# A decoder block on one core: down-projection terms at other places of the slot order, and four of eight weight sums of a unit made by accumulating DMAs

## The chip, the core and the metric

The kernel runs on one core of a Trainium2 chip. The metric is the device time of one execution in microseconds, as the median over runs of the same program. A profile of one further execution gives the time of every instruction on the five engines: PE (TensorE, matrix products, with PEld for its weight loads), ACT (ScalarE), DVE (VectorE), POOL (GpSimd) and SP (SyncE, which here issues the loads).

## The reference

One decoder layer over 256 tokens of width 1024, in float32: a mixer (eight causal block-sparse heads, four differential heads, two gates, an output projection) and then a gated feed-forward block. Only the second half is touched by the change:

```python
h = rms_norm(x, norm_ffn_pre_g[l])                                  # 256 x 1024
f = (jax.nn.silu(h @ w_gate[l]) * (h @ w_up[l])) @ w_down[l]        # w_gate, w_up: 1024 x 2816, w_down: 2816 x 1024
x = x + rms_norm(f, norm_ffn_post_g[l])
```

## The kernel before

**Products in three parts.** Each float32 operand is split into a high and a low part of a shorter type: ACT copies the raw tile to `whi`, DVE subtracts to get `wlo` (`split_part`, lines 183 and 186). One product is three matmuls, high by high, low by high, high by low (`mm3`, lines 215 to 217). A split piece of weights, usually 128 x 1024 numbers, is called a granule. Five pairs of buffers hold granules (`WB`); DVE, ACT and PE each work through their own queue in program order.

**The feed-forward block.** The 2816 columns are 22 blocks of 128, called f. Blocks 0 to 3 are done plainly (`nat_slots`). The other 18 come in six units, R and W by turns: `UNITS = [("R", 4), ("W", 6), ("R", 10), ("W", 12), ("R", 16), ("W", 18)]`.

- A unit R (`unit_R`) takes two blocks in eight slots on PE, four granules by two token tiles. The results go through silu and a product (`done`, line 1117, output `fr`).
- A unit W (`unit_W`) takes four blocks by a scheme of seven products in place of eight over halves of the inner dimension: it needs the weight pieces 11, 12, 21, 22 (gate and up, upper and lower half) and their sums T3 = 12 + 22, T1 = 11 + 12, T2 = 11 + T3, T4 = T2 + 21. Each piece is two pages of 128 x 1024, so there are eight sums per unit, all made on DVE (`job_add`, line 267). The loaded pages are `wpage`, and there are twelve of them for one unit.
- Each unit's result is turned over on PE and split again (`f_T`, lines 992, 997 and 999): the tile `fT`. Its PSUM bank "t" is a single one, so the next turn waits until DVE line 999 has read the bank.
- The down projection adds, for every block f, the product of `fT` with a granule of w_down into banks `acc` and `pv` (`z_slots`, two slots per block). These are the z slots. The last four blocks form the tail (`z_tail`).

**What sets the order.** PE's order is the list `slots`, written by hand near the end. Between slots, `run` lets ACT and DVE work ahead through the list of jobs (`todo`: splits, sums, and `s_step`, which forms the sums of activations that W needs), up to four granules and six slots ahead. SP issues a load (`load`) when the buffer that it goes to is given up; seven raw buffers and the pages turn over in the order of the jobs. In a unit R before, the slots stand so: two R slots, the turn of the last W unit's second result (`left`), two R slots, the z slots, four R slots; the turn of R's own result follows inside the next W, after that unit's first two slots.

Of the kernel before, what the change touches and what calls it, by code (L numbers as in the profile page):

```python
# [65 lines left out]
def tile_hybrid_block(  # L66
# [93 lines left out]

    def load(r):
        load_raw(r)
        for c, v in r["views"]:
            nc.sync.dma_start(r["tile"][:, :, c], v)

    def granule(n):
        g = gran[n]
# [84 lines left out]
    for kc in range(4):  # L252
        job_split(("un", kc), nr["un", kc], None if kc else (0, 1))

# [13 lines left out]

    def early_sums(f):

        def two(w, k0):
            return [raw_of([(slice(0, 512), rows(w, (k0 + 2 * i) * P, 2, f * P, 512))], 2, "page") for i in range(2)]

        b = wsum[f] = {"11": two(w_gate, 0), "12": two(w_up, 0), "21": two(w_gate, 4), "22": two(w_up, 4)}
        for n in ("T3", "T2"):
            b[n] = [raw_of([], 2, "page") for i in range(2)]
        b["T1"], b["T4"] = b["12"], b["21"]
        return [lambda d=d, x=x, y=y, i=i: job_add(b[d][i], b[x][i], b[y][i])  # L280
                for d, x, y in (("T3", "12", "22"), ("T1", "11", "12"), ("T2", "11", "T3")) for i in range(2)]

    def units_before(i):

# [3 lines left out]
        kb, fb = UNITS[i - 1]  # L288
        return list(range(fb, fb + (4 if kb == "W" else 2)))

    for ui, (kind, f0) in enumerate(UNITS):
        ds = [lambda i=i: job_split(("d", i), dr[i]) for i in units_before(ui)]
        if kind == "R":
            rr = [raw_of([(slice(0, 256), rows(w_gate, 2 * kc * P, 2, f0 * P, 256)),
                          (slice(256, 512), rows(w_up, 2 * kc * P, 2, f0 * P, 256))], 2) for kc in range(4)]
            rs = [lambda kc=kc: job_split(("r", f0, kc), rr[kc]) for kc in range(4)]
            ad = early_sums(UNITS[ui + 1][1])
            if ui == 0:
                sjobs = [raw_of([], 2, "page") for i in range(4)]

                def s_jobs(*ns):
                    def f():
                        if ns[0] == 0:
                            touch_s()
                        for n in ns:
                            add_job(lambda n=n: s_step(n))
                    return [f]

                def touch_s():
                    use(*sjobs)  # L310

                todo = s_jobs(0) + rs[0:1] + s_jobs(1) + rs[1:2] + s_jobs(2, 3) + ds[0:1] + s_jobs(4, 5) + ds[1:2] + \
                    s_jobs(6) + ds[2:3] + s_jobs(7, 8) + ds[3:4] + ad[0:1] + rs[2:3] + ad[1:3] + rs[3:4] + ad[3:]
            else:
                n = len(ds)
                todo = rs[0:2] + [x for i in range(n) for x in ds[i:i + 1] + ad[i:i + 1]] + rs[2:3] + ad[n:n + 1] + \
                    rs[3:4] + ad[n + 1:]
        else:
            b = wsum[f0]
            sp = {n: [lambda n=n, i=i: job_split((n, f0, i), b[n][i]) for i in range(2)]  # L320
                  for n in ("11", "21", "22", "T1", "T2", "T3", "T4")}
            t4 = [lambda i=i: job_add(b["T4"][i], b["T2"][i], b["21"][i]) for i in range(2)]
            todo = sp["21"] + sp["11"] + ds[0:1] + t4[0:1] + ds[1:2] + t4[1:2]
# [29 lines left out]
    def granules_ahead(slots, n, most):  # L353

        def f(i):
            j, seen = i + 1, set()
            while j < len(slots) and j - i <= most:
                seen |= {x for x, _ in slots[j]["need"]} - {x for x, _ in slots[i]["need"]}
# [189 lines left out]
    def ev_q(base):  # L548
        def f(c, a):
            q = work.tile([P, S], F32, tag="qf", name="q", bufs=2)  # L550
            nc.vector.tensor_tensor(q, a, R1, op=OP.mult)  # L551
            qhl = work.tile([P, 2, S], F32R, tag="q", name="q", bufs=5)
            qT[base + c] = (qhl[:, 0, :], qhl[:, 1, :])
            split(q, *qT[base + c])
        return f
# [429 lines left out]
    def f_T(fvs, f0, n, tag="t"):  # L985

        def pe():
            b = ps(tag)
            w = [(i, t, j) for i, t in enumerate(fvs) for j in range(n)]
            for i, t, j in w:  # L990
                c = (i * n + j) * P
                nc.tensor.transpose(b[:, c:c + P], fvs[t]()[:, j * P:(j + 1) * P], ident)
            h, l = [work.tile([P, 512], F32R, tag="q", name="fT", bufs=5) for _ in range(2)]
# [48 lines left out]
    def unit_W(f0):  # L1042
# [56 lines left out]
        return head, body[0], body[1], [f_T({1: lambda: st["f1"]}, f0, 4)]  # L1099

    def unit_R(f0):
        st = []

        def pe(kc, t):
            if not st:
                st.extend([dict(b=ps("s")), dict(b=ps("s"))])
            w = W(("r", f0, kc))
            for j in range(2):
                k = 2 * kc + j
                mm3(st[t]["b"], [v[:, k, t * P:(t + 1) * P] for v in (h2h, h2l)], [v[:, j, :] for v in w],  # L1110
                    start=k == 0, stop=k == KT - 1)
# [9 lines left out]
        return sl[0:2], sl[2:4], sl[4:8], [f_T({t: (lambda t=t: st[t]["f"]) for t in range(NT)}, f0, 2)]  # L1121

    def nat_slots():
        def pe(kc, t):
# [79 lines left out]
```

## Time and profile before

| | us |
|---|---|
| median of 3 runs (399.06 to 400.92) | 400.02 |
| the profiled execution, whole | 402.57 |
| its span, first to last instruction | 400.8 |
| PE busy in the span | 376.9 |
| DVE busy | 312.0 |
| ACT busy | 235.6 |
| POOL busy | 31.5 |

The time of the profiled execution is 1.8 us more than its span, and 2.55 us above the median of the runs. Busy time of PE counts each matmul with a modelled end, so gaps in it are read from the timeline of PE rather than from its share.

### The profile page before, as it was taken

What the parts mean: (1) busy time and instruction counts of PE and PEld (TensorE: products, weight loads), DVE (VectorE), ACT (ScalarE), POOL (GpSimd) and SP (SyncE); (2) the same over time, 40 slices, a digit from 0 to 9 for tenths busy, and PEclk for the clock granted to TensorE, in tenths of its full rate; (3) what the DMA queues carried; (4) which work ended last, traced back from release to release, by engine and by line L of the source; (5) the groups of instructions that cost most, each with busy time, mean ns of one, the idle gap of its engine ahead of it and who ended that gap; (6) DMA issues with size and microseconds to landing.
All of it is one profiled execution on the core that took longest, in us unless ns stands there. A gap on an engine that the chain in (4) does not pass through costs nothing.

```text
span 400.8 us, 6146 instructions
## 1 busy us (share of the span) xinstructions
PE 376.9 (94%) x2212; PEld 326.6 (81%) x2212; DVE 312.0 (78%) x556; ACT 235.6 (59%) x435; POOL 31.5 (8%) x51
## 2 busy tenths in 40 slices
PE   6999999999999999999999898998989989979693
PEld 4799989999999999998888677877868868756583
DVE  2699787999987577895787999689786898668724
ACT  3875675787665855653693455854465554628411
POOL 0099500000001000000000000000000000000000
PEclk9899999999999999999999999999999999989979
DMA  6969655252545744783399836666464753000002
GB/s 193 389 218 328 199 177 164 71 187 88 172 145 160 253 134 141 251 267 111 115 330 341 279 111 194 200 216 186 138 202 135 235 194 121 0 0 1 2 1 105
DMA packets 37857, 67.65 MB, mean 169 GB/s; under 512 B 2993, under 2 KB 15298, under 8 KB 37826
## 3 DMA queue, kind: packets, MB, share of 16 engines
q1 hardware_dynamic: 37826, 67.26, 51.4%
q8 instruction: 17, 0.28, 0.3%
q14 instruction: 14, 0.11, 0.1%
HBM read 66.20 MB, written 1.05 MB: 168 GB/s over the span
## 4 chain that ended last, share of the span: by engine, by line
PE 75%; DVE 11%; issue 5%; DMA 4%; ACT 4%; SPq 1%; DVEq 0%; POOLq 0%; ACTq 0%
PE acc L217 13%; PE acc L215 12%; PE acc L216 12%; PE s L215 7%; PE s L216 7%; PE s L217 7%; DVE wlo L186 5%; PE acc L612 4%; DMA wraw<-in_w_in_dram 3%; ACT whi L183 2%; PE pv L216 2%; PE pv L217 2%; PE pv L215 2%; DVE wpage L267 2%; DVE fT L999 1%
## 5 line engine op out<-in xcount | busy, mean ns | idle before, releaser
L186 DVE TENSOR_TENSOR wlo<-wraw,whi 128x512 fp32r<-128x512 f32 (+1 forms) x141 | 119.2, 868 | 29.4 <-ACT whi L183 29.1
L183 ACT ACTIVATE whi<-wraw 128x512 fp32r<-128x512 f32 (+1 forms) x140 | 101.6, 763 | 43.4 <-PE acc L216 14.5
L215 PE MATMUL acc<-hTh,whi 128*128 128x256 f32 x256 | 73.2, 286 | 0.4 <-DVE q L551 0.4
L217 PE MATMUL acc<-hTh,wlo 128*128 128x256 f32 x256 | 71.9, 281 | 0.0
L216 PE MATMUL acc<-hTl,whi 128*128 128x256 f32 x256 | 71.8, 281 | 0.0
L186 DVE TENSOR_TENSOR wlo<-wpage,whi 128x1024 fp32r<-128x1024 f32 x42 | 50.0, 1220 | 18.5 <-ACT whi L183 18.5
L183 ACT ACTIVATE whi<-wpage 128x1024 fp32r<-128x1024 f32 x42 | 43.5, 1058 | 29.3 <-PE pv L217 18.8
L215 PEld LDWEIGHTS acc<-hTh,whi 128*128 128x128 f32 x256 | 48.3, 189 | 0.7 <-DVE q L551 0.6
L216 PEld LDWEIGHTS acc<-hTl,whi 128*128 128x128 f32 x256 | 48.3, 189 | 0.0
L217 PEld LDWEIGHTS acc<-hTh,wlo 128*128 128x128 f32 x256 | 48.2, 188 | 0.0
L215 PE MATMUL s<-whi,h2h 128*128 128x512 f32 x92 | 37.6, 409 | 0.9 <-DVE v L1078 0.6
L217 PE MATMUL acc<-whi,fT 128*128 128x512 f32 (+1 forms) x80 | 30.6, 382 | 7.6 <-DVE fT L999 7.6
L216 PE MATMUL s<-wlo,h2h 128*128 128x512 f32 x92 | 36.4, 396 | 0.0
L217 PE MATMUL s<-whi,h2l 128*128 128x512 f32 x92 | 36.4, 395 | 0.0
L215 PE MATMUL acc<-whi,fT 128*128 128x512 f32 (+1 forms) x80 | 30.1, 377 | 0.0
L216 PE MATMUL acc<-wlo,fT 128*128 128x512 f32 (+1 forms) x80 | 30.0, 375 | 0.0
L267 DVE TENSOR_TENSOR wpage<-wpage 128x1024 f32<-128x1024 f32 x24 | 28.9, 1216 | 0.0
L217 PEld LDWEIGHTS acc<-whi,fT 128*128 128x128 f32 x80 | 15.6, 195 | 12.7 <-DVE fT L999 10.2
L215 PEld LDWEIGHTS s<-whi,h2h 128*128 128x128 f32 x92 | 17.3, 188 | 6.0 <-DVE fr L1117 1.6
L875 POOL TENSOR_TENSOR rs_r<-rs_e,mhalf 128x1 f32<-128x1 f32 x4 | 2.2, 546 | 241.1 <-DVE rs_e L874 241.1
L217 PEld LDWEIGHTS s<-whi,h2l 128*128 128x128 f32 x92 | 17.3, 188 | 4.2
L216 PEld LDWEIGHTS s<-wlo,h2h 128*128 128x128 f32 x92 | 17.3, 188 | 3.4
(267 smaller groups left out, 768.5 us busy)
## 6 DMA issues: line engine op xcount, KB each, us to landing
wraw<-in_w_in_dram SPq DMA_DIRECT2D x37, 512.0 KB, 4.9
wraw<-in_w_down_dram SPq DMA_DIRECT2D x22, 512.0 KB, 3.4
wpage<-in_w_up_dram SPq DMA_DIRECT2D x12, 512.0 KB, 4.1
wpage<-in_w_gate_dram SPq DMA_DIRECT2D x12, 512.0 KB, 4.1
wraw<-in_w_out_dram SPq DMA_DIRECT2D x8, 512.0 KB, 3.3
wraw<-in_w_gate_dram SPq DMA_DIRECT2D x12, 256.0 KB, 2.9
wraw<-in_w_up_dram SPq DMA_DIRECT2D x12, 256.0 KB, 3.9
wraw<-in_w_branch_a_dram SPq DMA_DIRECT2D x4, 512.0 KB, 4.3
```

The lines of the kernel that those rows point to most:

```text
L183: nc.scalar.activation(hi, src, AF.Copy)
L186: nc.vector.tensor_tensor(lo, src, hi.bitcast(F32), op=OP.subtract)
L215: nc.tensor.matmul(dst, lh, rh, start=start, stop=False, **kw)
L216: nc.tensor.matmul(dst, lh, rl, start=False, stop=False, **kw)
L217: nc.tensor.matmul(dst, ll, rh, start=False, stop=stop, **kw)
L267: nc.vector.tensor_tensor(dst["flat"], a["flat"], b["flat"], op=OP.add)
L612: nc.tensor.matmul(acc[t], l[:, k, ts_], r, start=k == 0 and n == 0, stop=k == KT - 1 and n == 2)
L875: nc.gpsimd.tensor_tensor(r[:, 0:1], e, mhalf, op=OP.pow)
L999: nc.vector.tensor_tensor(l, b, h.bitcast(F32), op=OP.subtract)
```

## The change

Three things. (1) The slots are placed otherwise: in a unit R all eight R slots stand together, with the turn of the last W's second result after the first two; then three z slots, the turn of R's own result, and the other z slots. In W the z slots stand where they stood, but nothing is turned ahead of them. At the end the turn of the last result comes after the first slot of the tail. (2) T3 and T1 are no longer sums on DVE: SP loads the first summand into a page and GpSimd's queue issues a DMA that adds the second one from HBM to it. Per unit SP then issues ten loads of 512 KB where it issued eight, and GpSimd's queue four: the pieces 11, 12 and 22 are read from HBM twice, and 12 has no page of its own. T2 and T4 stay on DVE. (3) The list of jobs follows (`braid` deals sums among splits; the three later granules of w_up for blocks 0 to 3 move into the first unit's list), the tail's granules are whole ones and all four sit in freed pages, and the tag "q" has six buffers instead of five.

```diff
     def load(r):
         load_raw(r)
+        seen = []
         for c, v in r["views"]:
-            nc.sync.dma_start(r["tile"][:, :, c], v)
+            if c in seen:
+                nc.gpsimd.dma_start(r["tile"][:, :, c], v, accum_op=OP.add)
+            else:
+                nc.sync.dma_start(r["tile"][:, :, c], v)
+            seen.append(c)
...
-        b = wsum[f] = {"11": two(w_gate, 0), "12": two(w_up, 0), "21": two(w_gate, 4), "22": two(w_up, 4)}
-        for n in ("T3", "T2"):
-            b[n] = [raw_of([], 2, "page") for i in range(2)]
-        b["T1"], b["T4"] = b["12"], b["21"]
-        return [lambda d=d, x=x, y=y, i=i: job_add(b[d][i], b[x][i], b[y][i])
-                for d, x, y in (("T3", "12", "22"), ("T1", "11", "12"), ("T2", "11", "T3")) for i in range(2)]
+        b = wsum[f] = {"11": two((w_gate, 0)), "T3": two((w_up, 0), (w_up, 4)), "T2": two(),
+                       "21": two((w_gate, 4)), "T1": two((w_gate, 0), (w_up, 0)), "22": two((w_up, 4))}
+        b["T4"] = b["21"]
+        return [lambda i=i: job_add(b["T2"][i], b["11"][i], b["T3"][i]) for i in range(2)]
...
-                n = len(ds)
-                todo = rs[0:2] + [x for i in range(n) for x in ds[i:i + 1] + ad[i:i + 1]] + rs[2:3] + ad[n:n + 1] + \
-                    rs[3:4] + ad[n + 1:]
+                todo = braid(rs + ds, ad)
+                rest = []
...
-    for h in range(2):
-        for f in range(NFF - NTAIL, NFF):
-            job_split(("d", f), dr[f], (h,))
+    for f in range(NFF - NTAIL, NFF):
+        job_split(("d", f), dr[f])
...
-    for f in range(NFF - 2, NFF):
+    for f in range(NFF - NTAIL, NFF):
         place[("d", f)] = in_free
...
-        if i == len(UNITS) - 1:
-            slots += a + left + b + zs[0:2] + c + zs[2:4] + nxt
+        if kind == "R":
+            sl, tr = unit_R(f0)
+            slots += sl[0:2] + left + sl[2:] + zs[0:3] + tr + zs[3:]
+            left = []
         else:
-            slots += a + left + b + zs + c
-        left = nxt
+            a, b, left = unit_W(f0)
+            slots += a + zs[0:2] + (zs[2:] + b if i < len(UNITS) - 1 else b + zs[2:])
...
-    slots += t0 + t1
+    slots += t0[0:1] + left + t0[1:] + t1
```

PE in the second unit R (blocks 10 and 11), before, from the turn of the preceding W's second result (`f_3290`) on; `s` are the unit's own banks, `acc` those of the down projection:

```order
L992 MATMUL t<-ident,f_3290 128x128 x4
L215 MATMUL s<-whi,h2h 128x512
L216 MATMUL s<-wlo,h2h 128x512
L217 MATMUL s<-whi,h2l 128x512
...
L217 MATMUL s<-whi,h2l 128x512
L215 MATMUL acc<-whi,fT 128x512
L216 MATMUL acc<-wlo,fT 128x512
L217 MATMUL acc<-whi,fT 128x512
```

The same place of the change, from the turn of the same result:

```order
L1000 MATMUL t<-ident,f_3298 128x128 x4
L220 MATMUL s<-whi,h2h 128x512
L221 MATMUL s<-wlo,h2h 128x512
L222 MATMUL s<-whi,h2l 128x512
...
L222 MATMUL s<-whi,h2l 128x512
L220 MATMUL acc<-whi,fT 128x512
L221 MATMUL acc<-wlo,fT 128x512
L222 MATMUL acc<-whi,fT 128x512
```

Between the turn and the first product with `fT` stood 12 matmuls, and now 36 stand there.

DVE in the third unit R (blocks 16 and 17), before, from the split of the preceding W's first result (line 999) on; line 267 is a sum of pages, line 186 the split of a granule:

```order
L999 TENSOR_TENSOR fT<-t,fT 128x512
L267 TENSOR_TENSOR wpage<-wpage 128x1024
L186 TENSOR_TENSOR wlo<-wraw,whi 128x1024
L267 TENSOR_TENSOR wpage<-wpage 128x1024
L186 TENSOR_TENSOR wlo<-wraw,whi 128x1024
L999 TENSOR_TENSOR fT<-t,fT 128x512
L267 TENSOR_TENSOR wpage<-wpage 128x1024
L186 TENSOR_TENSOR wlo<-wraw,whi 128x1024
L267 TENSOR_TENSOR wpage<-wpage 128x1024
L186 TENSOR_TENSOR wlo<-wraw,whi 128x1024
L267 TENSOR_TENSOR wpage<-wpage 128x1024
```

And of the change:

```order
L1007 TENSOR_TENSOR fT<-t,fT 128x512
L191 TENSOR_TENSOR wlo<-wraw,whi 128x1024
L271 TENSOR_TENSOR wpage<-wpage 128x1024
L191 TENSOR_TENSOR wlo<-wraw,whi 128x1024
L1007 TENSOR_TENSOR fT<-t,fT 128x512
L191 TENSOR_TENSOR wlo<-wraw,whi 128x1024 x2
L1125 TENSOR_TENSOR fr<-s,fr 128x256 x2
L191 TENSOR_TENSOR wlo<-wraw,whi 128x1024
L271 TENSOR_TENSOR wpage<-wpage 128x1024
L191 TENSOR_TENSOR wlo<-wpage,whi 128x1024 x2
L1007 TENSOR_TENSOR fT<-t,fT 128x512
```

Four instructions stood between the first two splits of `fT` and three stand there now; the sums in the unit went from six to two, and `fr` and its own `fT` come earlier.

POOL from the attention's last norm on, before (lines 432 and 875 are the power functions of the norms; `rs_2743` is the norm ahead of the feed-forward block):

```order
L432 TENSOR_TENSOR rs_r<-rs_e,mhalf 128x2 x4
L875 TENSOR_TENSOR rs_r<-rs_e,mhalf 128x1 x2
L432 TENSOR_TENSOR rs_2743<-rs_e,mhalf 128x2
L875 TENSOR_TENSOR rs_r<-rs_e,mhalf 128x1 x2
L1200 UNCONDITIONAL_BRANCH
```

And of the change:

```order
L440 TENSOR_TENSOR rs_r<-rs_e,mhalf 128x2 x4
L883 TENSOR_TENSOR rs_r<-rs_e,mhalf 128x1 x2
L166 DMA wpage<-in_w_up_dram 128x2x512
L440 TENSOR_TENSOR rs_2746<-rs_e,mhalf 128x2
L166 DMA wpage<-in_w_up_dram 128x2x512 x11
L883 TENSOR_TENSOR rs_r<-rs_e,mhalf 128x1 x2
```

Twelve accumulating DMAs now stand on POOL, one of them ahead of the norm that all silu functions of the block use, the others ahead of the last two norms.

## Rows read from the trace of the kernel before

**Rows 1.** Page, part 1: busy us (share of the span) and instructions of each engine.

```profile
PE 376.9 (94%) x2212; PEld 326.6 (81%) x2212; DVE 312.0 (78%) x556; ACT 235.6 (59%) x435; POOL 31.5 (8%) x51
```

**Rows 2.** Timeline of PE, 220 to 381: start, us, operation, [idle before <-releaser].

```profile
222.94 0.50 PE L217 MATMUL acc<-whi,fT 128*128 128x512 f32 x1 [1.49 <-DVE fT L999]
...
239.77 0.49 PE L215 MATMUL s<-whi,h2h 128*128 128x512 f32 x1 [0.38 <-DVE fr L1117]
...
247.64 0.50 PE L217 MATMUL acc<-whi,fT 128*128 128x512 f32 x1 [1.10 <-DVE fT L999]
...
271.13 0.66 PE L992 MATMUL t<-ident,f 128*128 128x128 f32 x4 [0.95 <-DVE fT L999]
...
276.27 0.50 PE L217 MATMUL acc<-whi,fT 128*128 128x512 f32 x1 [0.52 <-DVE fT L999]
...
300.32 0.50 PE L217 MATMUL acc<-whi,fT 128*128 128x512 f32 x1 [1.44 <-DVE fT L999]
...
323.88 0.66 PE L992 MATMUL t<-ident,f 128*128 128x128 f32 x4 [0.95 <-DVE fT L999]
...
329.02 0.50 PE L217 MATMUL acc<-whi,fT 128*128 128x512 f32 x1 [0.53 <-DVE fT L999]
...
351.02 0.39 PE L215 MATMUL acc<-whi,fT 128*128 128x512 f32 x1
351.24 0.40 PE L216 MATMUL acc<-wlo,fT 128*128 128x512 f32 x1
354.22 0.50 PE L217 MATMUL acc<-whi,fT 128*128 128x512 f32 x1 [2.58 <-DVE fT L999]
...
370.53 0.47 PE L215 MATMUL s<-whi,h2h 128*128 128x512 f32 x1 [0.56 <-DVE v L1078]
...
380.29 1.12 PE L992 MATMUL t<-ident,f 128*128 128x128 f32 x4 [3.50 <-DVE fT L999]
```

**Rows 3.** Busy time by stretch: PE, PEld, DVE, ACT, POOL, granted clock, DMA share, GB/s.

```profile
200.00:340.00 140.00, 132.64 (x628) 107.06 (x626) 118.47 (x121) 80.62 (x93) 0.69 (x1) 1.00 0.63 207
220.00:230.00 10.00, 8.51 (x44) 6.87 (x43) 10.00 (x11) 4.75 (x6) 0.00 (x0) 1.00 0.86 280
350.00:360.00 10.00, 7.42 (x29) 5.89 (x28) 6.21 (x7) 3.48 (x4) 0.00 (x0) 0.83 0.00 0
380.00:390.00 10.00, 9.71 (x33) 7.92 (x34) 1.80 (x5) 1.97 (x5) 0.00 (x0) 0.70 0.00 1
```

**Rows 4.** Timeline of DVE, 362 to 380, in the last unit W.

```profile
362.66 7.12 DVE L186 TENSOR_TENSOR wlo<-wpage,whi 128x1024 fp32r<-128x1024 f32 x6 [1.75 <-ACT whi L183]
...
371.63 1.29 DVE L186 TENSOR_TENSOR wlo<-wraw,whi 128x512 fp32r<-128x512 f32 x2
...
377.75 1.28 DVE L186 TENSOR_TENSOR wextra<-wraw,wextra 128x512 fp32r<-128x512 f32 x2
378.95 0.68 DVE L1091 TENSOR_TENSOR f<-f,v 128x512 f32<-128x512 f32 x1
379.56 0.68 DVE L999 TENSOR_TENSOR fT<-t,fT 128x512 fp32r<-128x512 f32 x1
```

**Rows 5.** Page, part 5: the group of the sums on DVE.

```profile
L267 DVE TENSOR_TENSOR wpage<-wpage 128x1024 f32<-128x1024 f32 x24 | 28.9, 1216 | 0.0
```

**Rows 6.** Loads issued from 196.9 to 197.9: issue ns, starts, and time to landing.

```profile
L164 SPq DMA_DIRECT2D wpage<-in_w_up_dram x2: 419/440/461, 196.9 to 197.3; - x2
DMA to landing us min/median/max: 6.4/6.8/7.2
```

**Rows 7.** Page, parts 3 and 6: the queue of the loads and one of its groups.

```profile
q1 hardware_dynamic: 37826, 67.26, 51.4%
...
wpage<-in_w_up_dram SPq DMA_DIRECT2D x12, 512.0 KB, 4.1
```

**Rows 8.** Timelines of POOL and of ACT, at the norm of the feed-forward block.

```profile
202.79 0.69 POOL L432 TENSOR_TENSOR rs<-rs_e,mhalf 128x2 f32<-128x2 f32 x1 [10.06 <-ACT whi L183]
...
206.00 1.27 ACT L1139 ACTIVATE fgs<-s,rs 128x512 f32<-128x512 f32 x2
```

More of the change, by code (lines that the diff above doesn't have):

```diff
@@ L251, in tile_hybrid_block @@
         job_split(("gn", kc), nr["gn", kc], (0, 1))
-    for kc in range(4):
-        job_split(("un", kc), nr["un", kc], None if kc else (0, 1))
+    job_split(("un", 0), nr["un", 0], (0, 1))
     NTAIL = 4
@@ L271, in early_sums, with two @@
     def early_sums(f):
-        def two(w, k0):
-            return [raw_of([(slice(0, 512), rows(w, (k0 + 2 * i) * P, 2, f * P, 512))], 2, "page") for i in range(2)]
-        b = wsum[f] = {"11": two(w_gate, 0), "12": two(w_up, 0), "21": two(w_gate, 4), "22": two(w_up, 4)}
-        for n in ("T3", "T2"):
-            b[n] = [raw_of([], 2, "page") for i in range(2)]
-        b["T1"], b["T4"] = b["12"], b["21"]
-        return [lambda d=d, x=x, y=y, i=i: job_add(b[d][i], b[x][i], b[y][i])
-                for d, x, y in (("T3", "12", "22"), ("T1", "11", "12"), ("T2", "11", "T3")) for i in range(2)]
+        def two(*wk):
+            return [raw_of([(slice(0, 512), rows(w, (k0 + 2 * i) * P, 2, f * P, 512)) for w, k0 in wk], 2, "page")
+                    for i in range(2)]
+        b = wsum[f] = {"11": two((w_gate, 0)), "T3": two((w_up, 0), (w_up, 4)), "T2": two(),
+                       "21": two((w_gate, 4)), "T1": two((w_gate, 0), (w_up, 0)), "22": two((w_up, 4))}
+        b["T4"] = b["21"]
+        return [lambda i=i: job_add(b["T2"][i], b["11"][i], b["T3"][i]) for i in range(2)]
     def units_before(i):
@@ L289, in units_before, with s_jobs, f, braid @@
         return list(range(fb, fb + (4 if kb == "W" else 2)))
+    sjobs = [raw_of([], 2, "page") for i in range(4)]
+    def s_jobs(*ns):
+        def f():
+            if ns[0] == 0:
+                use(*sjobs)
+            for n in ns:
+                add_job(lambda n=n: s_step(n))
+        return [f]
+    def braid(a, b):
+        n, o = len(a), []
+        for i in range(n):
+            o += a[i:i + 1] + b[len(b) * i // n:len(b) * (i + 1) // n]
+        return o
     for ui, (kind, f0) in enumerate(UNITS):
@@ L298, in tile_hybrid_block @@
             if ui == 0:
[L299 to L313, printed above, removed]
-            else:
-                n = len(ds)
-                todo = rs[0:2] + [x for i in range(n) for x in ds[i:i + 1] + ad[i:i + 1]] + rs[2:3] + ad[n:n + 1] + \
-                    rs[3:4] + ad[n + 1:]
+                uns = [lambda kc=kc: job_split(("un", kc), nr["un", kc]) for kc in range(1, 4)]
+                todo = uns[0:1] + s_jobs(0) + uns[1:2] + s_jobs(1) + uns[2:3] + s_jobs(2, 3, 4, 5) + rs[0:2] + \
+                    s_jobs(6) + rs[2:3] + s_jobs(7, 8) + rs[3:4] + braid(ds, ad[0:4])
+                rest = ad[4:]
+            else:
+                todo = braid(rs + ds, ad)
+                rest = []
         else:
@@ L322, in tile_hybrid_block @@
             t4 = [lambda i=i: job_add(b["T4"][i], b["T2"][i], b["21"][i]) for i in range(2)]
-            todo = sp["21"] + sp["11"] + ds[0:1] + t4[0:1] + ds[1:2] + t4[1:2]
+            todo = sp["21"] + sp["11"] + rest[0:1] + ds[0:1] + t4[0:1] + rest[1:2] + ds[1:2] + t4[1:2]
             for n in ("T2", "T1", "T3", "22", "T4"):
@@ L357, in f @@
             while j < len(slots) and j - i <= most:
-                seen |= {x for x, _ in slots[j]["need"]} - {x for x, _ in slots[i]["need"]}
+                seen |= {x for x, _ in slots[j]["need"] if x not in place} - {x for x, _ in slots[i]["need"]}
                 if len(seen) > n:
@@ L551, in f @@
             nc.vector.tensor_tensor(q, a, R1, op=OP.mult)
-            qhl = work.tile([P, 2, S], F32R, tag="q", name="q", bufs=5)
+            qhl = work.tile([P, 2, S], F32R, tag="q", name="q", bufs=6)
             qT[base + c] = (qhl[:, 0, :], qhl[:, 1, :])
@@ L992, in pe @@
                 nc.tensor.transpose(b[:, c:c + P], fvs[t]()[:, j * P:(j + 1) * P], ident)
-            h, l = [work.tile([P, 512], F32R, tag="q", name="fT", bufs=5) for _ in range(2)]
+            h, l = [work.tile([P, 512], F32R, tag="q", name="fT", bufs=6) for _ in range(2)]
             for i, t, j in w:
@@ L1098, in unit_W @@
         body[1].append(f_T({0: lambda: st["f0"]}, f0, 4))
-        return head, body[0], body[1], [f_T({1: lambda: st["f1"]}, f0, 4)]
+        return head + body[0], body[1], [f_T({1: lambda: st["f1"]}, f0, 4)]
     def unit_R(f0):
@@ L1120, in unit_R @@
                    post=[lambda t=t: active.append(done(t))] if kc == 3 else []) for kc in range(4) for t in range(NT)]
-        return sl[0:2], sl[2:4], sl[4:8], [f_T({t: (lambda t=t: st[t]["f"]) for t in range(NT)}, f0, 2)]
+        return sl, [f_T({t: (lambda t=t: st[t]["f"]) for t in range(NT)}, f0, 2)]
     def nat_slots():
@@ L1147, in tile_hybrid_block @@
     for i, (kind, f0) in enumerate(UNITS):
-        a, b, c, nxt = unit_W(f0) if kind == "W" else unit_R(f0)
         zs = [s for f in units_before(i) for s in z_slots("d", f, f_of, NFF - 1)]
-        if i == len(UNITS) - 1:
-            slots += a + left + b + zs[0:2] + c + zs[2:4] + nxt
-        else:
-            slots += a + left + b + zs + c
-        left = nxt
+        if kind == "R":
+            sl, tr = unit_R(f0)
+            slots += sl[0:2] + left + sl[2:] + zs[0:3] + tr + zs[3:]
+            left = []
+        else:
+            a, b, left = unit_W(f0)
+            slots += a + zs[0:2] + (zs[2:] + b if i < len(UNITS) - 1 else b + zs[2:])
     tail = list(range(NFF - NTAIL, NFF))
```

## The prediction

> **What bounds the kernel now.** I read the busy shares first: PE is busy for 376.9 of 400.8 us and the other engines for much less [rows 1]. So the kernel can get shorter where PE stands still, where its clock is down, or by fewer matmuls; the change has the same matmuls. Next I went through PE's timeline for every wait above 0.3 us. From 36 to 222 us there is none. From there on are eleven, and with one exception (the last but one, a bank of the unit W that DVE has yet to read) they end on DVE's splits of a unit's result or on its product `fr` [rows 2]. They add up to 1.49 + 0.38 + 1.10 + 0.95 + 0.52 + 1.44 + 0.95 + 0.53 + 2.58 + 0.56 + 3.50 = 14.0 us. Third, the table by stretch: the granted clock is 1.00 between 200 and 340, but 0.83 in the ten us with the wait of 2.58 us and 0.70 in the ten behind the wait of 3.50 us [rows 3]. Those are mixtures of PE's two levels, 2.4 and 1.2 GHz.
>
> Why are the splits late? They are short (0.68 us), but they stand in DVE's queue behind sums and splits of weights, and PE asks for them soon: in a unit R two R slots, 12 matmuls, after the turn. Behind the first such place DVE is busy for all of 10 us [rows 3]; at the end DVE works off a row of splits of the tail before the product `f` at 378.95 and the split at 379.56 that PE awaits [rows 4].
>
> **The change part by part.** The forecast is made on the profiled execution, 402.57 us, which is 2.55 above the median; I take the saving off the median.
>
> *The places of the z slots.* The waits ahead of `acc` at 222.94, 276.27 and 329.02 lie in units R. There now are 36 matmuls between the turn and the z slots instead of 12. From the rows at 351.02 and 351.24, one follows the other after 0.22 us [rows 2], so 24 more give 5.3 us, more than each of the waits 1.49, 0.52 and 0.53. The waits at 247.64, 300.32 and 354.22 belong to `fT` of a unit R, used in the next W. Its turn moves ahead of five z slots (6 or 9 matmuls each, as much work as an R slot of 6 x 0.23 = 1.4 us: 7 us) and stands before four W slots in place of two (2.8 us more); about 10 us of cover against 1.10, 1.44 and 2.58. The wait at 239.77 is for a bank that the product `fr` gives back; eight z slots, some 11 us, now lie ahead of it. All seven go: 1.49 + 0.52 + 0.53 + 1.10 + 1.44 + 2.58 + 0.38 = 8.04 us.
>
> *The tail.* The 3.50 us at 380.29 come from eight half splits of the tail that stand on DVE between the first result's product, done at 371.6, and `f` [rows 4]. PE began to wait at 376.8, behind a turn (0.4 us) and two z slots (2.8 us); the first turn thus stood at 373.6. The change splits whole granules, two ahead of the first result's product and two between it and `f`, and puts one tail slot more ahead of the second turn. A whole granule is 1.2 us on DVE (twice 0.6 [rows 4]). So the first product comes at 371.6 + 2.4 = 374.0, and the turn 0.4 late; then two splits, `f` and `fT`, 2.4 + 0.7 + 0.7, are done at 377.8, while PE has turned and done its two z slots at 374.0 + 0.4 + 2.8 = 377.2 and waits 0.6 for the first tail slot. About 1.0 us of new waits, and 2.5 of the 3.5 go.
>
> *Which stay.* The two waits of 0.95 us are for the bank "t" between the first and the second turn of a W. What stands ahead of them on DVE and PE is the same as before; I leave them. So is the bank wait of 0.56.
>
> *What each wait costs besides its idle time.* The matmul at 354.22 starts 2.98 us behind the one before it, 0.22 would be its pace; 2.76 against an idle of 2.58, so 0.15 to 0.2 more than the row prints [rows 2]. Eight waits: 1.2 us.
>
> *The clock.* A granted mean of 0.83 over 10 us is 3.4 us at half rate, in which the work of 1.7 us is lost; 0.70 over 10 us loses 3.0, of which 0.2 fell into the wait itself [rows 3]. Both stretches lie directly behind the two longest waits; behind waits up to 1.49 us the clock stayed at 1.00 [rows 2, 3]. If the long ones go, 4.5 us come back.
>
> *The sums.* Twelve sums of 1,216 ns leave DVE, 14.6 us [rows 5]. PE is never held by DVE's total (118.47 of 140 us [rows 3]), so this counts for nothing directly. It is what lets DVE run ahead in units R. It costs loads: per unit two more from SP and four accumulating ones, 18 in all. By the queue, 67.26 MB took 51.4% of 400.8 us, 206 us, so 512 KB take 1.6 us of all sixteen DMA engines [rows 7]. Six more plain loads are 10 us. An accumulating DMA is not in this trace. Below: as a plain load, 1.6 us of the engines and 4.1 us to landing. Above: it also reads its target and starts when the first summand has landed; I bound it by four times the first, 6.4 us, and by two of the longest landings, 14 us [rows 6, 7]. In 200 to 340 the DMA share is 0.63, so 52 us are free [rows 3], 45 when the stage is 6 to 7 us shorter; less 10 for the plain loads, 35 remain for twelve: 2.9 us each fit without any delay. I take twice a plain load, 3.2 us: 38 us, which fits almost, and what does not fit goes into the time after 340, since by 350 nothing is loaded any more [rows 3]. In time: T3 is wanted by a sum of DVE near 224 in the first unit, its first summand is issued at about 197 and lands like the loads of that time after 6.4 to 7.2 us [rows 6], so some 20 us are left for the second, against 7 to 14. Value: 0.
>
> *POOL.* The norm ahead of silu, at 202.79, now stands behind the first accumulating DMA, which waits for that load: 197.3 + 6.4 to 7.2 = 204 to 204.5, plus its own issue. No row has an issue on POOL; SP's takes 0.42 to 0.46 [rows 6], and with the norm's 0.69 [rows 8] the result is there at about 206, where ACT asks for it at 206.00 [rows 8]. If the issue took 4 us, ACT would be held to 209; its next splits are for the first R slots at 214, so that too costs PE nothing. Value: 0.
>
> A rule speaks against this part. On this path the trace shows only that DVE is busy without a gap for up to 10 us at a stretch [rows 3]. The Trainium skill ("SBUF — State Buffer", section "SBUF: two separate sides") says that GpSimd can't write the descriptors of its own DMAs while VectorE runs an operation in a two-port mode, so that such a DMA seems to be blocked by VectorE. Whether these sums and splits are such operations no run here shows yet; by it the sum would be that of the third rival below.
>
> **Sum.** 8.0 + 2.5 + 1.2 + 4.5 = 16.2 us: 402.6 becomes 386.4, and the median 400.0 becomes 383.8. I say 384.
>
> **The rivals.**
>
> 1. *The waits move.* The z slots are free, but PE meets new waits of a microsecond at the bank "t", at the splits of d (DVE's order in R is now r, r, r, r, d, d, d, d) or at the tail, and one of them is long enough for the clock to drop again. For it: the two waits of 0.95 stay as they are. Against it: DVE has 14.6 us less to do [rows 5]. Price: half of the waits and one of the two clock drops come back, 8 us: 392.
> 2. *Slower: the loads bind.* An R and a W together take 52.7 us (247.64 to 300.32 [rows 2]), 49 without their waits. In that time the engines of the DMAs have to carry 20 plain loads, 32 us, and four accumulating ones; if one of those takes c us, the sum fits up to c = 4.2. Beyond it two and a half periods lose 10 (c - 4.2), less some 15 us of lead, since the pages of T1 are given up in one W and wanted in the next, behind a unit R of 16 slots. To eat the 16 us gained, c must pass 7.3, over four times a plain load. At c = 9: 48 - 15 = 33 us lost against 16 gained, so 417. For it: no row shows the operation. Against it: only reading the target is added to what a load does.
> 3. *GpSimd's queue starves.* The issue of each accumulating DMA waits for a gap of DVE, at most about 10 us [rows 3], and the norm behind the first one waits with it. Held from 204 to 214, the norm makes silu and the first R slots 5 us late; the other units have that much lead. Price: 5 us, and 2 for the clock: 391. It is the rule of the Trainium skill named above ("SBUF — State Buffer") as a mechanism of this kernel.
> 4. *Nothing happens.* DVE is late for another reason, ACT's high parts, for which it waits 1.75 us at the head of [rows 4], and z slots wait wherever they stand: 400.
>
> **How the numbers follow.** The forecast gets 0.70 (381.5 to 387: down to the sum with the waits of 0.56 and 0.95 gone too, up to it with 3 us of new waits), rival 1 0.14, rival 2 0.07, rival 3 0.05, rival 4 0.04. The range 381 to 392 holds the forecast and half or more of rivals 1 and 3, some 0.8. A change of this kernel can be told from none at about 0.5%, 2 us; faster by more than that is the forecast, rival 1 and rival 3, 0.88; same 0.04; slower 0.08.
>
> **What would show it.** In the profile of the changed kernel PE's timeline has no wait ahead of `acc<-whi,fT` in units R and W, and two of about 1 us ahead of the turn of a W's second result. The clock is 1.00 from 200 to 375. In the tail one wait of half to one us. DVE's group of sums has 12 in place of 24. The accumulating DMAs land in under 15 us and no engine's list of waits names them. The norm on POOL starts between 204.5 and 207. Wrong I would be if PE waits for splits of `wpage` at T1 or T3, if DVE's sum of T2 waits for a DMA, or if the clock falls in a place where no long wait stands before it.

## The result and the profile after

The changed kernel takes 384.51 us, median of 4 runs (384.02 to 384.85); beside it the kernel before takes 400.25 (399.06 to 400.92, now four runs). The ratio is 0.9609, 95% interval 0.9583 to 0.9635. The forecast was 384, the range 381 to 392. The profiled execution took 384.85 us with a span of 383.1; it is compared here with the profiled one of before, 402.57 and 400.8. The lines of the code moved by some: a matmul of a product is now line 220 to 222, the split 191, a sum of pages 271, the turn 1000, the split of a turned result 1007.

Busy time of the engines, the two queues that carry the weights, and two groups of DMA issues, from the page of the changed kernel (a queue's row: packets, MB, share of sixteen engines; an issue's row: KB each, us to landing):

```profile
PE 369.6 (96%) x2212; PEld 322.8 (84%) x2212; DVE 298.1 (78%) x540; ACT 234.2 (61%) x431; POOL 47.1 (12%) x63
...
q1 hardware_dynamic: 39458, 70.40, 54.9%
q0 software_dynamic: 3264, 6.29, 9.1%
...
L166 POOL DMA_DIRECT2D wpage<-in_w_up_dram x12 | 14.6, 1220 | 106.7 <-DMA wpage<-in_w_up_dram 43.3
...
wpage<-in_w_up_dram SPq DMA_DIRECT2D x12, 512.0 KB, 7.4
wpage<-in_w_up_dram POOLq DMA_DIRECT2D x12, 512.0 KB, 9.9
```

PE has the same 2212 matmuls and 7.3 us less busy time [rows 1]: they are not fewer, but more of them ran at the higher clock: the mean granted clock is 0.997 in this execution and was 0.982 in that of before, which by (1 - 0.982) of 400.8 us and (1 - 0.997) of 383.1 us is 6 us at full rate. DVE lost 13.9 us, close to the 14.6 of the twelve sums [rows 5]. The new queue used 9.1% of 383.1 us on all engines, 34.9 us for twelve DMAs, 2.9 us each.

PE's waits in the timeline of the changed kernel, all above 0.2 us from 36 us on:

```profile
266.80 0.66 PE L1000 MATMUL t<-ident,f 128*128 128x128 f32 x4 [0.95 <-DVE fT L1007]
...
316.66 0.66 PE L1000 MATMUL t<-ident,f 128*128 128x128 f32 x4 [0.95 <-DVE fT L1007]
...
348.61 0.50 PE L220 MATMUL s<-whi,S 128*128 128x512 f32 x1 [0.21 <-DVE g L1071]
...
358.17 0.47 PE L220 MATMUL s<-whi,h2h 128*128 128x512 f32 x1 [0.57 <-DVE v L1086]
...
361.76 0.63 PE L1000 MATMUL t<-ident,f 128*128 128x128 f32 x4 [0.56 <-DVE f L1092]
```

No row has `acc<-whi,fT` any more. Of eleven waits, 14.0 us in all [rows 2], five are left with 3.24 us; three of them (twice 0.95, and the one for `v`) are the ones of before. 10.8 us of waits are gone.

Busy time by stretch (PE, PEld, DVE, ACT, POOL, granted clock, DMA share, GB/s):

```profile
200.00:340.00 140.00, 138.09 (x661) 113.57 (x660) 109.78 (x114) 84.02 (x98) 16.19 (x13) 1.00 0.90 276
...
350.00:360.00 10.00, 9.36 (x40) 6.98 (x39) 9.66 (x9) 9.76 (x12) 0.00 (x0) 1.00 0.00 1
...
360.00:370.00 10.00, 9.44 (x49) 7.64 (x48) 5.90 (x10) 2.58 (x5) 0.00 (x0) 1.00 0.01 2
370.00:380.00 10.00, 6.78 (x42) 5.83 (x40) 6.15 (x14) 2.33 (x8) 1.11 (x2) 1.00 0.17 61
```

Where before the clock fell to 0.83 and 0.70 [rows 3] it stays at 1.00. The DMA share in 200 to 340 rose from 0.63 to 0.90.

### The profile page after: what moved, and what is told of

The parts are those of the page before. It is cut to its first block, busy times and chain, and to the rows that moved or that the text cites. A ratio compares the mean times of both kernels' runs of the same rounds, so it can differ in the third digit from the quotient of the medians.

```text
span 383.1 us, 6164 instructions
## 1 busy us (share of the span) xinstructions
PE 369.6 (96%) x2212; PEld 322.8 (84%) x2212; DVE 298.1 (78%) x540; ACT 234.2 (61%) x431; POOL 47.1 (12%) x63
## 3 DMA queue, kind: packets, MB, share of 16 engines
q1 hardware_dynamic: 39458, 70.40, 54.9%
## 4 chain that ended last, share of the span: by engine, by line
PE 87%; DVE 5%; issue 2%; DMA 2%; ACT 1%; SPq 1%; DVEq 0%; POOLq 0%; ACTq 0%
PE acc L220 14%; PE acc L221 14%; PE acc L222 14%; PE s L220 9%; PE s L221 9%; PE s L222 9%; PE acc L620 5%; DVE wlo L191 2%; PE pv L221 2%; PE pv L222 2%; PE pv L220 2%; DMA xt<-in_x_dram 2%; ACT whi L188 1%; PE t L1000 1%; PE t L221 1%
## 5 line engine op out<-in xcount | busy, mean ns | idle before, releaser
L191 DVE TENSOR_TENSOR wlo<-wraw,whi 128x512 fp32r<-128x512 f32 (+1 forms) x137 | 116.7, 874 | 37.4 <-ACT whi L188 36.8
L188 ACT ACTIVATE whi<-wraw 128x512 fp32r<-128x512 f32 (+1 forms) x136 | 99.1, 766 | 36.9 <-PE acc L221 14.5
L166 POOL DMA_DIRECT2D wpage<-in_w_up_dram x12 | 14.6, 1220 | 106.7 <-DMA wpage<-in_w_up_dram 43.3
L220 PE MATMUL acc<-whi,fT 128*128 128x512 f32 x72 | 26.5, 369 | 0.0
L222 PE MATMUL acc<-whi,fT 128*128 128x512 f32 x72 | 26.2, 364 | 0.0
L221 PE MATMUL acc<-wlo,fT 128*128 128x512 f32 x72 | 26.2, 363 | 0.0
L220 PE MATMUL s<-whi,S 128*128 128x512 f32 x48 | 19.2, 399 | 0.3 <-DVE g L1071 0.2
L222 PE MATMUL s<-whi,S 128*128 128x512 f32 x48 | 19.0, 395 | 0.0
```

The source lines that it names most:

```text
L166: nc.gpsimd.dma_start(r["tile"][:, :, c], v, accum_op=OP.add)
L188: nc.scalar.activation(hi, src, AF.Copy)
L191: nc.vector.tensor_tensor(lo, src, hi.bitcast(F32), op=OP.subtract)
L220: nc.tensor.matmul(dst, lh, rh, start=start, stop=False, **kw)
L221: nc.tensor.matmul(dst, lh, rl, start=False, stop=False, **kw)
L222: nc.tensor.matmul(dst, ll, rh, start=False, stop=stop, **kw)
```

## The experiments

Each is named by its change. Times are medians of its runs, ratios are to the kernel before, run on the same chip beside it. As a yardstick, the changed kernel was run a second time beside experiments 3, 7 and 8; there it took 384.24 us (383.91 to 385.58), ratio 0.9606 (0.957 to 0.9642).

**1. The slots without the accumulating DMAs.** The changed kernel, but with T3 and T1 as sums on DVE.

```diff
-        b = wsum[f] = {"11": two((w_gate, 0)), "T3": two((w_up, 0), (w_up, 4)), "T2": two(),
-                       "21": two((w_gate, 4)), "T1": two((w_gate, 0), (w_up, 0)), "22": two((w_up, 4))}
+        b = wsum[f] = {"11": two(w_gate, 0), "12": two(w_up, 0), "21": two(w_gate, 4), "22": two(w_up, 4)}
...
+                for d, x, y in (("T3", "12", "22"), ("T1", "11", "12"), ("T2", "11", "T3")) for i in range(2)]
```

> The changed kernel with all eight sums of a unit made on DVE again (no accumulating DMA); slots and jobs as in the change. Theory (the waits went because the z slots stand farther behind the turns, and the sums on DVE only use up time that DVE has): 384.5 to 386, no wait of PE ahead of acc<-whi,fT. Rival (DVE's relief by 14.6 us is what made the splits come in time): half of the gain goes, 390 or more, with PE waits on DVE line 1007 in units R.

Measured: 383.82 us (383.65 to 384.24), ratio 0.9600 (0.9568 to 0.9631). That is the whole gain, 0.7 us better than the range expected, and PE's waits are those of the changed kernel, although DVE is busy for 13 us more. The list of jobs, the splits of the tail and the look-ahead (which in the change no longer counts granules that go to freed pages) are those of the change here, so the time alone doesn't tell them from the slots. The timelines do. In the second unit R the split of W's second result on DVE and the first z slot on PE, in the kernel before (the turn is at 271.13 [rows 2]):

```profile
275.53 0.68 DVE L999 TENSOR_TENSOR fT<-t,fT 128x512 fp32r<-128x512 f32 x1
...
274.43 0.40 PE L215 MATMUL acc<-whi,fT 128*128 128x512 f32 x1
```

and here the turn, the split and the first z slot:

```profile
266.00 0.66 PE L1000 MATMUL t<-ident,f 128*128 128x128 f32 x4 [0.95 <-DVE fT L1007]
...
270.41 0.68 DVE L1007 TENSOR_TENSOR fT<-t,fT 128x512 fp32r<-128x512 f32 x1
...
274.90 0.40 PE L220 MATMUL acc<-whi,fT 128*128 128x512 f32 x1
```

In both kernels the split is done 5.1 us after the turn starts; the z slots begin 3.3 us after it before, and 8.9 us here. So this split comes no sooner; PE asks for it later. For R's own turn the same two figures are 5.3 and 3.3 us before (second unit R) and 4.3 and 13.0 us here: there the split is 1.0 us sooner, and PE asks 9.7 us later.

**2. The accumulating DMAs alone.** The kernel before, with the diff's `load` and its two sums per unit, the slots as before.

```diff
             if c in seen:
+                nc.gpsimd.dma_start(r["tile"][:, :, c], v, accum_op=OP.add)
...
+        return [lambda i=i: job_add(b["T2"][i], b["11"][i], b["T3"][i]) for i in range(2)]
```

> The kernel before with T3 and T1 made by accumulating DMAs; slots, turns and tail as before. Theory: the sums that stand between the turns and the z slots are few, so the waits nearly all stay: 398 to 400. Rival (DVE's relief does it): 392 or less.

Measured: 400.65 us (398.07 to 402.94), ratio 1.0009 (0.9979 to 1.0040). No gain, not even the small one that I had expected. In its timeline PE waits as before; only the 0.38 is gone. The groups of DVE's waits between 200 and 340 (in total, times, longest) say why. First the kernel before:

```profile
DVE wlo L186 <- ACT whi L183: 18.4, 18, 1.9
```

and the kernel of this experiment, with three of PE's waits from its timeline, two in units W and one at the tail, and the stretch behind the last:

```profile
DVE wlo L191 <- ACT whi L188: 32.3, 28, 1.9
```

```profile
246.84 0.50 PE L222 MATMUL acc<-whi,fT 128*128 128x512 f32 x1 [1.43 <-DVE fT L1004]
...
353.29 0.50 PE L222 MATMUL acc<-whi,fT 128*128 128x512 f32 x1 [2.56 <-DVE fT L1004]
...
379.13 1.11 PE L997 MATMUL t<-ident,f 128*128 128x128 f32 x4 [3.51 <-DVE fT L1004]
...
380.00:390.00 10.00, 10.00 (x45) 8.27 (x44) 3.81 (x8) 2.52 (x7) 0.57 (x1) 0.90 0.01 6
```

DVE's busy time in this stretch fell by 13.1 us (118.47 [rows 3] to 105.36), and its waits for ACT's high parts grew by 13.9. The freed time went into waits, and the splits that PE awaits came no earlier: the one in the second unit R is done 5.1 us after its turn starts, as before. The reason I read from the code: how far ACT and DVE may look ahead is bound to PE's slots. In line with it, ACT waits in this stretch 23.9 us for PE to be done with `pv`, where it was 20.2.

**3. The accumulating DMAs left out.** The changed kernel without these twelve DMAs.

```diff
-                nc.gpsimd.dma_start(r["tile"][:, :, c], v, accum_op=OP.add)
+                pass
```

> The changed kernel without its twelve accumulating DMAs; T3 and T1 are then only their first summands, so these sums are left out. Theory (they lie wholly beside other work): the same time as the changed kernel within 0.5 us, with some 35 us less of DMA time between 200 and 340. Rival (they slow other loads or the norm on POOL that stands behind the first one): 0.7 us or more faster.

Measured: 384.30 us (384.07 to 384.73), ratio 0.9603 (0.9564 to 0.9641). The same as with them, with a DMA share of 0.69 in place of 0.90 between 200 and 340: as they stand they cost nothing, and they give nothing (experiments 1 and 2).

**4. R's turn back in W.** The changed kernel, with the turn of R's result again behind the first two slots of the next W, and all z slots of R behind its R slots.

```diff
-            slots += sl[0:2] + left + sl[2:] + zs[0:3] + tr + zs[3:]
-            left = []
+            slots += sl[0:2] + left + sl[2:] + zs
+            left = tr
...
+            a, left = a[0:2] + left + a[2:], nxt
```

> The changed kernel with the turn of R's result back where it was, behind the first two slots of the next W. Theory: the waits of the three units W come back, 1.10 + 1.44 + 2.58 with 0.5 for three restarts, and in some runs the clock falls behind the longest: 389 to 392. Rival (DVE, with fewer sums to do, has the split ready in time): 386 or less.

Measured: 390.05 us (389.02 to 390.60), ratio 0.9735 (0.9692 to 0.9778), as expected. The waits ahead of the z slots of W are back, and only those:

```profile
243.51 0.50 PE L222 MATMUL acc<-whi,fT 128*128 128x512 f32 x1 [1.06 <-DVE fT L1007]
...
294.67 0.50 PE L222 MATMUL acc<-whi,fT 128*128 128x512 f32 x1 [1.06 <-DVE fT L1007]
...
346.88 0.64 PE L222 MATMUL acc<-whi,fT 128*128 128x512 f32 x1 [2.20 <-DVE fT L1007]
```

The three add up to 4.32 us (5.12 in [rows 2]); the time rose by 5.8 over 384.24. The rest fits the restarts and the clock, which is 0.85 in the ten us around the last of these waits:

```profile
340.00:350.00 10.00, 7.80 (x31) 5.91 (x30) 7.95 (x8) 4.83 (x6) 0.00 (x0) 0.85 0.00 0
```

**5. The tail as before.** The changed kernel, with half splits, two of four granules in freed pages, and the last turn ahead of the tail.

```diff
-    for f in range(NFF - NTAIL, NFF):
-        job_split(("d", f), dr[f])
+    for h in range(2):
+        for f in range(NFF - NTAIL, NFF):
+            job_split(("d", f), dr[f], (h,))
...
-    slots += t0[0:1] + left + t0[1:] + t1
+    slots += left + t0 + t1
```

> The changed kernel with the tail of before: half splits of the last four granules of w_down, two of them in the ordinary buffers, and the turn of the last result ahead of the first tail slot. Theory: the wait of about 3.5 us comes back in place of 1.1 us, and the clock falls behind it, which costs another 2.5 to 3: 389 to 390.5, with a granted clock near 0.7 in the ten us behind the wait. Rival (the clock of before fell for another reason, such as what stood ahead of the tail): 387, clock 1.00.

Measured: 385.80 us (four runs: 385.56, 385.77, 385.84, 389.42), ratio 0.9669 (0.9622 to 0.9715). I was wrong by some 4 us. The wait is back, but shorter than 3.50, and the clock behind it stays at 1.00 in the profile:

```profile
365.51 0.66 PE L1001 MATMUL t<-ident,f 128*128 128x128 f32 x4 [2.13 <-DVE fT L1008]
```

The reason is in ACT's queue. Timelines of DVE and of ACT in the kernel before, at the tail's half splits:

```profile
371.63 1.29 DVE L186 TENSOR_TENSOR wlo<-wraw,whi 128x512 fp32r<-128x512 f32 x2
375.33 1.29 DVE L186 TENSOR_TENSOR wextra<-wraw,wextra 128x512 fp32r<-128x512 f32 x2 [2.42 <-ACT wextra L183]
...
373.61 0.69 ACT L1089 ACTIVATE f<-s,rs 128x512 f32<-128x512 f32 x1 [2.97 <-PE s L217]
...
374.67 1.15 ACT L183 ACTIVATE wextra<-wraw 128x512 fp32r<-128x512 f32 x2
```

and in this experiment:

```profile
357.14 1.14 ACT L188 ACTIVATE wextra<-wraw 128x512 fp32r<-128x512 f32 x2
360.19 0.69 ACT L1098 ACTIVATE f<-s,rs 128x512 f32<-128x512 f32 x1 [1.92 <-PE s L222]
...
358.22 1.28 DVE L191 TENSOR_TENSOR wlo<-wraw,whi 128x512 fp32r<-128x512 f32 x2
...
364.17 0.68 DVE L1100 TENSOR_TENSOR f<-f,v 128x512 f32<-128x512 f32 x1
```

Before, the second pair of high parts stands on ACT behind `f`, which waits 2.97 us for PE, and DVE idles 2.42 us for it. Here it stands ahead of `f`. From the first of the eight half splits to `f` on DVE are 5.95 us, before 378.95 - 371.63 = 7.32 [rows 4]: 1.37 less, and just so much shorter is PE's wait. The edit thus did not restore the tail of before; the other order of the slots had also moved the tail's jobs on ACT. The clock came out as my rival had it, and that a wait of this length lowers the clock is not shown. The one run of 389.42 had a mean granted clock of 0.989, the other three 0.996 to 0.998; no trace shows where in that run the clock was down.

**6. A later turn of W's second result.** The changed kernel; in the second and third unit R the turn stands behind four R slots in place of two.

```diff
-            slots += sl[0:2] + left + sl[2:] + zs[0:3] + tr + zs[3:]
+            slots += sl[0:2] + left + sl[2:] + zs[0:3] + tr + zs[3:] if i == 0 else sl[0:4] + left + sl[4:] + zs[0:3] + tr + zs[3:]
```

> The changed kernel with the turn of a W's second result after four R slots instead of two, in the second and the third unit R. Theory: the two waits of 0.95 us for the bank go with about 0.2 us of restart each, and nothing takes their place, since four R slots (5.6 us) still lie between the turn and the z slots: 382.0 to 382.8. Rival (the second result's split now comes too late for the z slots, behind more splits on DVE): 384 or more, with a wait ahead of acc<-whi,fT.

Measured: 382.06 us (381.78 to 382.39), ratio 0.9554 (0.9526 to 0.9583), as expected: the two waits of 0.95 us, which the change had left, are gone.

**7. Both without DMA sums.** Experiment 1 with the edit of experiment 6.

> All eight sums on DVE (no accumulating DMA) and the turn of a W's second result after four R slots in the second and third unit R. Theory (the sums on DVE cost nothing in this order, and the bank waits go as they did with the accumulating DMAs): 381.3 to 382.1. Rival (DVE, with 13 us more to do, is now late for the splits behind the later turn): 383 or more, with a wait ahead of acc<-whi,fT.

Measured: 381.99 us (381.39 to 382.29), ratio 0.9543 (0.9508 to 0.9579).

**8. The results ahead of the tail's splits.** Experiment 7, and around T4 of the last W the list of jobs runs ahead by five and then by three slots instead of six, so that DVE makes W's last products before it splits more of the tail.

```diff
-    run(slots, granules_ahead(slots, WB - 1, 6))
+    far, near = granules_ahead(slots, WB - 1, 6), [granules_ahead(slots, WB - 1, m) for m in (5, 3)]
+    t4 = [i for i, s in enumerate(slots) if any(x == ("T4", UNITS[-1][1], 0) for x, _ in s["need"])][0]
+    run(slots, lambda i: far(i) if i < t4 - 1 else near[i > t4](i))
```

> As the run with sums on DVE and the later turn; besides, ACT and DVE look less far ahead in the last W, so that the unit's two results come before the tail's splits on DVE. Theory: the wait of 0.56 us ahead of the first turn goes with its restart, about 0.7 us less than that run; 380.6 to 381.4. The wait of 0.56 for the unit's bank stays. Rival (the tail's splits now come too late for the first tail slots): the same or slower, with a wait ahead of acc<-wextra,fT.

Measured: 381.09 us (380.92 to 381.63), ratio 0.9525 (0.9490 to 0.9560). This is the best version of the study, 3.15 us below the changed kernel run beside it, with eight sums of every unit on DVE and 67.26 MB in the loads' queue as before. Behind 200 us PE has two waits left:

```profile
345.61 0.50 PE L220 MATMUL s<-whi,S 128*128 128x512 f32 x1 [0.21 <-DVE g L1071]
...
355.17 0.47 PE L220 MATMUL s<-whi,h2h 128*128 128x512 f32 x1 [0.56 <-DVE v L1086]
```

**9. Each accumulating DMA twice.** The changed kernel; it asks how much more than the 2.9 us the loads would bear.

```diff
-                nc.gpsimd.dma_start(r["tile"][:, :, c], v, accum_op=OP.add)
+                for _ in range(2):
+                    nc.gpsimd.dma_start(r["tile"][:, :, c], v, accum_op=OP.add)
```

> The changed kernel with each of the twelve accumulating DMAs issued a second time behind the first (the second summand is then added twice, so T3 and T1 are changed). In the profile of the changed kernel one takes 2.9 us of the sixteen engines, two take 5.8. Theory (the sums of my second rival: 4.2 us fit in a period, and what is beyond loses 10 (5.8 - 4.2) less 15 of lead): 384 to 387. Rival (the engines of the DMAs, busy for 0.90 of 200 to 340, have no such room): 390 or more, with PE waiting behind splits of wpage.

Measured: 405.23 us (401.83 to 406.45), ratio 1.0122 (1.0085 to 1.0159): 1.2% slower than the kernel before, and 18 us above the top of my estimate. The timelines of POOL, ACT and PE in the first unit:

```profile
203.62 1.39 POOL L167 DMA_DIRECT2D wpage<-in_w_up_dram  x1 [12.32 <-DMA wpage<-in_w_up_dram]
215.93 1.20 POOL L167 DMA_DIRECT2D wpage<-in_w_up_dram  x1 [10.92 <-DMA wpage<-in_w_up_dram]
216.68 1.20 POOL L441 TENSOR_TENSOR rs<-rs_e,mhalf 128x2 f32<-128x2 f32 x1
...
217.92 1.27 ACT L1148 ACTIVATE fgs<-s,rs 128x512 f32<-128x512 f32 x2 [13.34 <-POOL rs L441]
...
220.18 0.80 PE L221 MATMUL s<-whi,h2h 128*128 128x512 f32 x1 [7.11 <-ACT whi L189]
...
265.61 0.80 PE L221 MATMUL s<-whi,S 128*128 128x512 f32 x1 [3.87 <-ACT whi L189]
```

The second DMA to a page waits at the head of POOL's queue until the first has landed; the norm stands behind it, and ACT waits for the norm. At 265.61 PE waits for a page of the first unit W, for which ACT waits 7.35 us. The clock was 0.77 in 220 to 230 and 0.78 in 260 to 270.

**10. Twice in the later units only.** The same, from the second unit W on.

```diff
+    twice = []
...
-                nc.gpsimd.dma_start(r["tile"][:, :, c], v, accum_op=OP.add)
+                twice.append(c)
+                for _ in range(2 if len(twice) > 4 else 1):
+                    nc.gpsimd.dma_start(r["tile"][:, :, c], v, accum_op=OP.add)
```

> The changed kernel with the eight accumulating DMAs of the second and third unit W issued twice, and the four of the first unit once (in the two later units T3 and T1 contain their second summand twice). Where all twelve were issued twice the time was 405.2 us. If that loss lay wholly in the first unit (there the second DMA stood ahead of the norm on GpSimd's queue, and the pages of its own T1 and T2 came late), this kernel stays within 0.5% of the changed one: 383 to 386 us, no PE wait on a load, although the queue has to carry eight more accumulating DMAs of some 3 us of the sixteen engines each. Rival: the later units have no room either; then PE waits for whi of a page between 290 and 370 and the time is 390 us or more.

Measured: 387.94 us (387.34 to 390.45), ratio 0.9734 (0.9676 to 0.9792), between what the two theories gave. Some four fifths of the loss of experiment 9 lie in the first unit, (405.2 - 387.9) of (405.2 - 384.2) us, though this run was on another chip than the other two; but the later ones are not free either. The queue of the accumulating DMAs, POOL's group of issues, in the timelines POOL, ACT and PE in the last unit W, and the stretch with PE's wait:

```profile
q0 software_dynamic: 5440, 10.49, 15.2%
...
L170 POOL DMA_DIRECT2D wpage<-in_w_up_dram x20 | 24.4, 1341 | 126.7 <-DMA wpage<-in_w_up_dram 95.7
...
342.31 1.20 POOL L170 DMA_DIRECT2D wpage<-in_w_up_dram  x1 [6.21 <-DMA wpage<-in_w_up_dram]
...
348.14 1.06 ACT L192 ACTIVATE whi<-wpage 128x1024 fp32r<-128x1024 f32 x1 [4.28 <-DMA wpage<-in_w_up_dram]
...
351.11 0.50 PE L224 MATMUL s<-whi,S 128*128 128x512 f32 x1 [3.28 <-DVE g L1075]
...
350.00:360.00 10.00, 8.81 (x36) 6.59 (x36) 8.22 (x9) 8.91 (x11) 0.00 (x0) 1.00 0.00 1
```

The last one is issued at 342.31; in the changed kernel the last started at 313.8. PE's wait of 3.28 us, which was 0.21 in the changed kernel, makes up 3.1 of the 3.7 us lost. POOL sat 95.7 us waiting for what goes to the same page to land, 52.7 of them for an earlier accumulating DMA; in the changed kernel it was 43.3, all for plain loads. The DMA share between 200 and 340 was 1.02. Whether the engines or the chain of landings in POOL's queue set the 342.31 these runs don't tell apart.

## Why the prediction was right, step by step

- **The places of the z slots: right.** All seven waits (8.04 us) went, as the timeline of the changed kernel shows; experiment 4 brings back those that it undoes, and experiment 1 shows that it needs no accumulating DMA, and by its timelines that PE asks much later while the splits come little or no sooner.
- **The waits that stay: right.** Twice 0.95 and the one for `v`, 0.57 where it was 0.56, are there. Not foreseen was the small one of 0.21 ahead of a bank of the last W.
- **The tail: nearly right.** One wait of 0.56 at the first turn (0.4 was worked out) and none ahead of the first tail slot (0.6 was). The splits and products of DVE that I added up by their durations start closer behind one another: two whole granules at 361.54, `f` 2.27 us later, `fT` 0.60 after that. So 2.9 of 3.5 us went, not 2.5. What the step had wrong in part was its reason: the row of eight half splits held 2.42 us in which DVE waited for ACT, and experiment 5 shows that about 1.4 of the 3.5 us go by ACT's order alone, without the new tail. Undoing the tail costs 1.6 us (385.80 against 384.24).
- **Waits together:** 10.8 us of idle time against 8.04 + 2.5 = 10.5.
- **The clock: the term was too large for the medians, somewhat small for the profiled run, and its reason is not shown.** The runs of the kernel before differ by it: of those beside experiment 10 the ones with a mean granted clock of 0.997 took 397.32 and 397.34 us, those with 0.984 and 0.986 400.79 and 401.19. The profiled execution had 0.982 and took 402.57, which is 5.3 us above them where I had 4.5. The changed kernel's median of 384.5 comes from runs at 0.995 to 0.998. At about the same mean clock the change is thus worth 397.3 - 384.5 = 12.8 us, the waits and restarts, for which I had 8.0 + 2.5 + 1.2 = 11.7; for the clock 400.25 - 397.3 = 2.9 us remain between the medians, where I had 4.5. Taking a saving read from one execution with much loss off the median of the others put 1.6 us too many in, and the waits 1.1 too few: the forecast came out within 0.5 us partly by luck, through two errors of opposite sign. Nor does the length of a wait settle whether the clock falls, as the step assumed. The wait of 3.28 us in experiment 10 left it at 1.00, that of 2.20 in experiment 4 went with 0.85; behind 3.50 us it was 0.70 [rows 3], behind 3.51 in experiment 2 it was 0.90. The runs show that kernels with the long waits lose clock in many executions and the changed kernel in few; what decides it in one execution stays open.
- **The sums on DVE: right that they count for nothing, wrong in the sentence that their going lets DVE run ahead in units R.** It hardly does: in the changed kernel the split of the second unit R is done 4.1 us after its turn starts and not 5.1 (266.80 to 270.90), which PE no longer needs; experiments 1 and 3 give times within 0.7 us of the changed kernel's, with them and without, and in experiment 2 the freed time turned into DVE's waits for ACT.
- **The accumulating DMAs: 2.9 us of the engines against 3.2 taken**, inside the bounds of 1.6 and 6.4; landing 7.7 to 13.7 us against up to 14. Nothing in the trace waits for one of them.
- **POOL's norm: the start was in the forecast window, the end was not.** In the timeline of the changed kernel:

```profile
204.49 1.39 POOL L166 DMA_DIRECT2D wpage<-in_w_up_dram  x1 [12.36 <-DMA wpage<-in_w_up_dram]
205.44 1.98 POOL L440 TENSOR_TENSOR rs<-rs_e,mhalf 128x2 f32<-128x2 f32 x1
```

  Its result came at 207.4 and not at 206; ACT waited 2.1 us for it and PE not at all, which the bound with an issue of 4 us had covered. Experiment 9 shows where this cover ends: with the norm done at 217.9 PE lost 7.1 us at once.
- **Rival 1 (the waits move)** did not come: 0.21 and 0.56 are all that is new.
- **Rival 2 (the loads bind)** did not come, since c was 2.9. But its threshold was wrong. Two DMAs in place of one make c about 6, for which its formula, 10 (c - 4.2) - 15, gives 3 us; 21 were lost. It counted engines and a lead of 15 us, which the later units roughly have (experiment 10: 3.7 us lost) and the first has not: there the norm stands in GpSimd's queue behind the second DMA, and PE lost 7.1 us at it and 3.9 at a page of the first W.
- **Rival 3 (GpSimd's queue starves)** did not come. The first of the twelve issues took 1385 ns, the others 1203 to 1230, while DVE was busy for 8.6 of every 10 us in 210 to 230, with sums and splits that the trace lists as TENSOR_TENSOR. The rule of the Trainium skill ("SBUF — State Buffer", section "SBUF: two separate sides") thus bore on nothing here; that these sums and splits are operations in a two-port mode remains unshown.
- **Rival 4 (nothing)** is what experiment 2 measured for the second part of the change taken alone.

## What to carry to other kernels

Where PE waits for a short step that stands in another engine's queue, put other work of PE between the step and its use; here 24 matmuls more ended a wait that 13 us less work on the other engine left untouched. Before moving work off an engine, see what that engine waits for: if its lead is bound to PE's place in the program, the freed time only becomes another wait. And read a saving from an execution with the same granted clock as the runs that it is taken off.

## What was not expected of the hardware

- The norm on POOL took 1.98 us directly behind a DMA issue on the same engine, 1.20 and 1.25 in experiments 9 and 10, and 0.69 without one [rows 8]. Its span starts at 205.44, before that of the issue ends (204.49 + 1.39), so part of it may be a wait for the issue.
- An accumulating DMA of 512 KB took 2.9 to 3.0 us of the sixteen engines in three kernels (34.9 us for 12; 15.2% of 385.6 us for 20; 17.9% of 401.2 for 24), against 210.3 us for 70.40 MB, 1.57 us for 512 KB, in the plain queue of the changed kernel. Its issue takes 1.2 us of POOL's time.
- The plain loads of w_up into `wpage` landed in a median of 7.4 us where it was 4.1 before [rows 7], and 5.4 with the accumulating DMAs left out (experiment 3): the engines' share in use went up to 0.90 over 140 us, and no wait of PE came of it.
- In experiment 5, with a wait of 2.13 us, one execution of four had a mean granted clock of 0.989 and took 3.6 us more than the others. In experiment 10 a wait of 3.28 us left the clock at 1.00.
